# The last feed-forward with 512-column products of the hi weights, its two halves added on the way out, and its operand rows 32 and 16 bytes further apart

## The chip, the cores and the metric

One core of a Trainium2 chip runs one launch of the program. The metric is the time of that launch on the device in microseconds (us), median of several runs. The engines are named as the profile names them: PE multiplies matrices, PEld is its loading of weights, DVE and ACT work on rows of elements and read the accumulators, POOL does a little arithmetic, SP issues the transfers from memory.

## The reference

One inference step of a two-layer diffusion backbone for two groups of 128 tokens each: a context pass and a denoising step with cached keys. Both groups use the same weights, so the kernel handles them as 256 columns side by side. A layer is a mixer (latent and grouped attention in layer 0, differential attention in layer 1) and then a gated feed-forward with a width-3 convolution over positions. The change lies in the feed-forward of layer 1:

```
h = rmsnorm(x, g_norm_ffn[l]) * (1 + sc2) + sh2
u = h @ w_up                                    # 2048 -> 2 * 5632
u = up[:, :-2] * w_conv[0] + up[:, 1:-1] * w_conv[1] + up[:, 2:] * w_conv[2] + b_conv
gate, val = u[..., :D_FF], u[..., D_FF:]
x = x + gt2 * ((silu(gate) * val) @ w_down)     # 5632 -> 2048
```

All arrays are float32.

## The kernel before

**Precision by halves.** A product of float32 numbers is made of three products of a shorter kind. Every operand is split into hi (rounded, by ACT) and lo (what is left, by DVE): `split`, L247 to L249. A block of 128 by 128 weights thus exists as `wh` and `wl`, a row of activations as 256 hi columns followed by 256 lo columns. A block's share of a product is three matmuls of 256 columns (`gemm`, L356 to L381): wh with the hi columns, wh with the lo columns, wl with the hi columns, all added up in one accumulator bank `acc`. In each of them the block of weights is the stationary operand and the activations stream. Each matmul has its own weight load, so wh of a block is loaded twice.

**Rows.** The modulated activations of the feed-forward are the tile `hx`: 16 rows of 512 float32 (`operand`, L729), 2048 bytes from one row's start to the next. The gated activations are tiles `g` of 512 float32, one tile for each row.

**The feed-forward** (`ffn`, from L1501). The hidden width of 5632 is handled in two halves (NQ = 2) of 22 blocks (KQ). For each half, `up(q)` makes 44 products of 16 blocks: a gate and a value for each of 22 rows. `conv` takes a product out of its accumulator: ACT scales it and adds the bias (L1531), DVE adds the two shifted terms (L1534, L1537), both reading the accumulator. Then come silu (L1553), the product with the gate (L1554) and the split into `g`. `down(gs, q)` makes 16 products of 22 blocks, and DVE adds each into the residual `x` (`residual`, L843; the very last one in `last_residual`, L827). Four products of layer 1's first half are there before `ffn` starts (`ready`). The first products that are made inside have their first matmul widened by 32, 16, 8, 4 and 2 columns (`WIDER`).

**Weights.** SP brings 1 MB of raw weights at a time into one of three buffers; ACT rounds 8 blocks (1024 columns) into one of four `wh` buffers (L248), DVE subtracts into one of four `wl` buffers (L249). A buffer is written again when PE has used it.

**Beside it.** While the feed-forward runs, DVE also sums conditioning vectors (`feature_step`, L473): 2048 columns at a time, 0.7 of them for each product of `up`, 32 of them in this feed-forward.

**Order.** A scheduler orders the instructions of each engine when the program is built; `keep_order` pins some of them. Accumulators rotate over three banks. The order in which PE takes products is fixed once built: near the turn from `up` to `down` it interleaves products so that the last gated row is asked for late.

Of the kernel before, what the change touches and what calls it, by code (L numbers as in the profile page):

```python
# [12 lines left out]
F32R = mybir.dt.float32r  # L13
AF = mybir.ActivationFunctionType
ALU = mybir.AluOpType
# [3 lines left out]
P = 128  # L19
D = 2048  # L20
KD = D // P
T = 128
NT = 2 * T
ROW = 2 * NT
SHIFT = 320
NL = 2
# [29 lines left out]
PEW = {"heads": 1.0, "out0": 1.0, "c": 1.0}  # L56
QUIET = [4, 3, 3]
LATE = 3

EARLY = (2, 5, 8, 11, 13)  # L60
WIDER = (32, 16, 8, 4, 2)
# [33 lines left out]
def step_kernel(ctx: ExitStack, tc: tile.TileContext, A: dict):  # L95
# [45 lines left out]
    def T_(pl, shape, tag, dt=F32, bufs=None):  # L141
        kw = {} if bufs is None else {"bufs": bufs}
        return pl.tile(shape, dt, tag=tag, name=nm(tag), **kw)
# [208 lines left out]
        return [p[:, :NT] for p in ps]  # L352

    push = []

    def gemm(blocks, xh, xl, n=NT, first=0, between=None, more=None, wider=None):  # L356

# [367 lines left out]
    def home(pl, tag):  # L725

        return T_(pl, [P, (KD * 2 * UW + 127) // 128 * 128], tag, F32R)

    def operand(pl, tag):  # L729
        return home(pl, tag)[:, :KD * ROW].rearrange("p (k n) -> p k n", k=KD)  # L730

    def raw_tile(pl, tag):
        return home(pl, tag)[:, :KD * 2 * UW].rearrange("p (k n) -> p k n", k=KD)
# [1 line left out]
    def modulated(st, l, which, W, u, to, rp, tag="block"):  # L735


        ensure(l, 3 * which + 1)
        ensure(l, 3 * which)
        while later:  # L740
            later.pop(0)()
        for q in range(4):
            raw_shift(u, l, which, q)
        unit = ROWS[ada["i"]] if ada["i"] < len(ROWS) else None
        raws, got = [], {}

        def load_tile():
            raw = T_(wpool, [P, 4, 512], "araw", bufs=2)
            sp.dma_start(out=raw, in_=A["w_ada"][unit[0], unit[1], unit[2], len(raws)])
            raws.append(raw)  # L750

        def stats():
            got["r"] = stat_rstd(st, D, att_bank)

        def factor():
            got["rb"] = spread(got["r"], bank=att_bank)

        def sums(t):
            for i in range(2):
                sum_rows(t + i, raws[t + i])  # L760
            if t == 0:
                load_tile()
                load_tile()
            else:
                ada["i"] += 1
                steps.extend(ada_finish(*unit))
                steps.pop(0)()

        hooks, steps = [{6: stats, 13: factor}, {}, {}], []
        if unit:  # L770
            load_tile()
            load_tile()
            hooks[1][6] = lambda: sums(0)
            hooks[2][13] = lambda: sums(2)
        else:
            hooks.append({})
        uh, ul = (lambda k: u[:, k, :UW]), (lambda k: u[:, k, UW:])
        ps = [gemm(W.chunk(), uh, ul, UW, between=hook) for hook in hooks[:-1]]
        last = W.chunk()
        rb = got["rb"]  # L780
        rbs = T_(tmp, [P, NT], "sq", bufs=2)
        act.copy(rbs, rb)
        hx = operand(*to)
        ready = [scaled(p, rbs) for p in ps]
        for c in range(KD):
            if c % 2 == 0:
                pair = T_(rp, [P, 512], tag, bufs=3)
            row(hx, rb, l, which, c, pair[:, c % 2 * NT:(c % 2 + 1) * NT])
            if c in (5, 10):
                W.ahead(lambda i: i)  # L790
        ready.append(scaled(gemm(last, uh, ul, UW, between=hooks[-1]), rbs))
        if which == 0:
            later.extend(steps)
            steps.clear()
        return hx, ready, [(lambda: steps.pop(0)(keep_order))] if steps else []
# [704 lines left out]

    def ffn(hx, W, ready, turn, l, st):  # L1501
        xh, xl = (lambda k: hx[:, k, :NT]), (lambda k: hx[:, k, NT:2 * NT])
        wider = list(WIDER)
        long = len(ready) > 3

        def product():
            if ready:
                return ready.pop(0)
            if in_order:
                return gemm(W.chunk(), xh, xl, between=in_order.pop(0))  # L1510
            if wider:
                n = NT + wider.pop(0)
                return gemm(W.chunk(), xh, xl, more=lambda k: hx[:, k, :n])
            return gemm(W.chunk(), xh, xl)
# [3 lines left out]
        with tc.tile_pool(name=f"ffn{l}", bufs=1) as fp, banks(f"pffn{l}") as pf:  # L1518
            feat["home"], feat["pool"] = fp, pf
            feat["due"] = 0.0  # L1520
            in_order = [{}, {}] + turn + [{}]
            T_(fp, [P, SHIFT // 4], "pad")

            def conv(m):
                early = bool(ready)
                pin = keep_order if early else lambda i: i
                if len(ready) > 4 - 2 * long:
                    W.ahead(pin)
                ps = product()
                y = T_(fp, [P, NT], "cv", bufs=3)  # L1530
                pin(act.activation(y, ps, AF.Identity, scale=cw[:, 1, m:m + 1], bias=cw[:, 3, m:m + 1]))  # L1531
                y3 = y.rearrange("p (g t) -> p g t", g=2)
# [11 lines left out]
            def up(q):  # L1544
                gs = []
                for i in range(q * KQ, (q + 1) * KQ):
# [5 lines left out]
                    pump(0, rate)  # L1552
                    act.activation(gate, gate, AF.Silu)  # L1553
                    dve.tensor_tensor(out=val, in0=gate, in1=val, op=ALU.mult)  # L1554
                    g = T_(fp, [P, ROW], "g", F32R, bufs=KQ)
                    split(g[:, :NT], g[:, NT:2 * NT], val)
                    gs.append(g)
                    if i == LATE - 1:
# [3 lines left out]
            def down(gs, q):  # L1562
# [4 lines left out]
                for c in range(KD):  # L1567
                    quiet = q == NQ - 1 and c >= KD - QUIET[0]
                    fine[0] = quiet
                    if q == 0:  # L1570
                        ensure(l, 5, [c // 4])
                    ps = gemm(WD.chunk(), lambda k: gs[k][:, :NT], lambda k: gs[k][:, NT:2 * NT])
                    if l == NL - 1 and q == NQ - 1 and c == KD - 1:
                        last_residual(ps, l, 1, c, st)
                    else:
# [205 lines left out]
```

## Time and profile before

| | us |
|---|---|
| time of a launch, median of 3 runs | 2306.41 (2305.07 to 2306.84) |
| span of the profiled execution | 2305.7 |
| layer 1's feed-forward in that profile | about 1590 to 2293 |
| PE busy over the span | 2275.9 |
| DVE busy over the span | 1885.6 |
| ACT busy over the span | 1195.7 |

The span is counted from the first to the last instruction of the profiled execution; it lies 0.7 us under the median of the runs, so a difference in span can be put onto the median. A row of a profile names the source line, the engine, the operation, output<-inputs by the program's names, and shapes; "x943" is how many. Matmuls overlap, so a matmul's listed duration (276 ns) is longer than its share of the time; the share is read from the starts, or from how many begin in a stretch. A busy share of 100% for PE says that it always had a matmul under way, not that it went as fast as it can.

### The profile page before, as it was taken

Reading aid. Unit: us, or ns where it says so; the run is one execution under the profiler, and the core shown is the slowest. Engines: PE = TensorE matmul, PEld = TensorE weight load, DVE = VectorE, ACT = ScalarE, POOL = GpSimd, SP = SyncE. Lnnn points to the kernel's source line nnn. Section 1 sums busy time; section 2 is a strip of 40 time slices with the busy share of each in tenths; the row PEclk is TensorE's granted clock in tenths of the full one; section 3 lists DMA queues with packets and bytes.
Section 4 is the critical chain, followed back from the end, with each engine's and each line's share of the span. In section 5 each row is a group of like instructions: output and inputs, shape, how many; then the busy total and the mean of one; then the engine's idle time right before and its main releaser. Section 6 shows DMA issues by size and latency. Waiting matters only on the chain.

```text
span 2305.7 us, 47484 instructions
## 1 busy us (share of the span) xinstructions
PE 2275.9 (99%) x19496; PEld 2182.1 (95%) x19496; DVE 1885.6 (82%) x2973; ACT 1195.7 (52%) x1959; POOL 188.1 (8%) x238
## 2 busy tenths in 40 slices
PE   8999999999999999999999999999999999999998
PEld 6788878999999999999999999999999999999998
DVE  4667979989999999999978988898899965666654
ACT  4345555665553355555575455457555434555543
POOL 0002111300000000001130001023000000000011
PEclk9999999999999999999999999999999999999999
DMA  9987888777777777777788888776667755555553
GB/s 376 367 343 293 326 311 338 288 277 264 262 255 291 291 272 260 272 258 258 288 293 293 318 322 310 267 268 229 246 256 262 264 200 189 199 191 194 198 189 126
DMA packets 100122, 617.15 MB, mean 268 GB/s; under 512 B 10752, under 2 KB 18880, under 8 KB 33344
## 3 DMA queue, kind: packets, MB, share of 16 engines
q1 hardware_dynamic: 99904, 614.11, 72.2%
q8 instruction: 153, 2.51, 0.4%
q14 instruction: 65, 0.53, 0.1%
HBM read 609.32 MB, written 4.75 MB: 266 GB/s over the span
## 4 chain that ended last, share of the span: by engine, by line
PE 93%; DVE 3%; DMA 2%; issue 1%; POOL 1%; ACT 1%; SPq 0%; DVEq 0%; ACTq 0%; POOLq 0%
PE acc L110 86%; PE ada L110 3%; PE att L110 2%; DVE wl L249 1%; DVE hx L525 1%; DMA more<-w_ada 1%; PE att L113 1%; DMA raw<-w_out_c 0%; PE misc L110 0%; DMA araw<-w_ada 0%; DMA kvb<-w_ada 0%; POOL dev L807 0%; PE ada L113 0%; DVE rope L858 0%; ACT wh L248 0%
## 5 line engine op out<-in xcount | busy, mean ns | idle before, releaser
L110 PE MATMUL acc<-hx,wh 128*128 128x256 f32 (+1 forms) x7264 | 1255.2, 278 | 4.2 <-ACT wh L248 1.7
L248 ACT CAST wh<-raw 128x1024 fp32r<-128x1024 f32 (+1 forms) x834 | 796.6, 967 | 869.8 <-PE acc L110 736.6
L249 DVE TENSOR_TENSOR wl<-raw,wh 128x1024 fp32r<-128x1024 f32 (+1 forms) x834 | 925.4, 1126 | 246.9 <-ACT wh L248 240.2
L110 PEld LDWEIGHTS acc<-hx,wh 128*128 128x128 f32 x7264 | 1099.8, 188 | 23.2 <-ACT wh L248 8.1
L110 PE MATMUL acc<-hx,wl 128*128 128x256 f32 (+1 forms) x3632 | 1007.8, 278 | 5.3 <-DVE wl L249 5.1
L110 PEld LDWEIGHTS acc<-hx,wl 128*128 128x128 f32 x3632 | 684.5, 188 | 9.5 <-DVE wl L249 6.9
L110 PE MATMUL acc<-g,wh 128*128 128x256 f32 x2816 | 478.8, 276 | 0.0
L110 PEld LDWEIGHTS acc<-g,wh 128*128 128x128 f32 x2816 | 424.0, 188 | 0.0
L110 PE MATMUL acc<-g,wl 128*128 128x256 f32 x1408 | 388.1, 276 | 0.0
L473 DVE CUSTOM_DVE_ANT_0 junk<-araw,condb 128x2048 f32<-128x2048 f32 x128 | 294.4, 2300 | 0.0
L110 PEld LDWEIGHTS acc<-g,wl 128*128 128x128 f32 x1408 | 264.2, 188 | 0.0
L211 POOL TENSOR_TENSOR sqacc<-sqacc,sq 128x256 f32<-128x256 f32 x62 | 71.5, 1154 | 1491.1 <-ACT sq L207 1490.9
L110 PE MATMUL acc<-hxc,wh 128*128 128x256 f32 (+1 forms) x1056 | 189.3, 281 | 0.0
L110 PEld LDWEIGHTS acc<-hxc,wh 128*128 128x128 f32 x1056 | 161.9, 188 | 1.8 <-issue 1.7
L110 PE MATMUL acc<-hxc,wl 128*128 128x256 f32 (+1 forms) x528 | 146.9, 278 | 0.0
L110 PEld LDWEIGHTS acc<-hxc,wl 128*128 128x128 f32 x528 | 99.6, 189 | 0.2
L110 PE MATMUL acc<-wh,hxc 128*128 128x256 f32 (+1 forms) x512 | 95.0, 283 | 0.5 <-DVE nt L818 0.5
L1531 ACT ACTIVATE cv<-acc,convw 128x256 f32<-128x256 f32 x169 | 94.1, 557 | 0.0
L525 DVE CUSTOM_DVE_ANT_0 hx<-block,condb 128x1024 fp32r<-128x1024 f32 x65 | 79.3, 1221 | 7.3 <-DMA block<-w_ada 6.8
L1537 DVE SCALAR_TENSOR_TENSOR cv<-acc,convw,cv 128x254 f32<-128x254 f32 x169 | 81.1, 480 | 3.2
L843 DVE SCALAR_TENSOR_TENSOR x<-acc,mod,x 128x128 f32<-128x128 f32 x190 | 57.3, 344 | 31.6 <-PE acc L110 31.6
L110 PEld LDWEIGHTS acc<-wh,hxc 128*128 128x128 f32 x512 | 79.4, 188 | 3.4 <-issue 2.5
(263 smaller groups left out, 1800.4 us busy)
## 6 DMA issues: line engine op xcount, KB each, us to landing
raw<-w_up SPq DMA_DIRECT2D x176, 1024.0 KB, 4.8
araw<-w_ada SPq DMA_DIRECT2D x136, 1024.0 KB, 6.0
raw<-w_down SPq DMA_DIRECT2D x88, 1024.0 KB, 4.8
raw<-w_in_c SPq DMA_DIRECT2D x48, 1024.0 KB, 6.9
block<-w_ada SPq DMA_DIRECT2D x41, 512.0 KB, 6.8
raw<-w_in_ab SPq DMA_DIRECT2D x18, 1024.0 KB, 9.1
raw<-w_out_ab SPq DMA_DIRECT2D x16, 1024.0 KB, 7.9
raw<-w_out_c SPq DMA_DIRECT2D x16, 1024.0 KB, 7.1
```

Of the source, the lines that this page charges most:

```text
L110: return self.placed(nc.tensor.matmul(*a, **kw))
L113: return self.placed(nc.tensor.transpose(*a, **kw))
L211: eng.tensor_tensor(out=st["acc"], in0=st["acc"], in1=sq, op=ALU.add)
L248: pin(act.copy(out_hi, src))
L249: pin(dve.tensor_tensor(out=out_lo, in0=src, in1=out_hi.bitcast(F32), op=ALU.subtract))
L473: keep_order(dve.tensor_tensor_reduce(out=T_(feat["pool"], [P, D], "junk"), in1=feat["row"][:, c], in0=feat["raw"].rearrange("p g n -> p ( ...
L525: keep_order(dve.tensor_tensor_reduce(out=self.junk, in0=self.raw, in1=self.row[:, c].rearrange("p (g n) -> p g n", g=2), scale=1.0, scala ...
L843: dve.scalar_tensor_tensor(out=x[:, c, s], in0=ps[:, s], scalar=mod[:, l, 3 * which + 2, c, g:g + 1], in1=x[:, c, s], op0=ALU.mult, op1=AL ...
L1531: pin(act.activation(y, ps, AF.Identity, scale=cw[:, 1, m:m + 1], bias=cw[:, 3, m:m + 1]))
L1537: pin(dve.scalar_tensor_tensor(out=y3[:, :, :T - 1], in0=p3[:, :, 1:], scalar=cw[:, 2, m:m + 1], in1=y3[:, :, :T - 1], op0=ALU.mult, op1=A ...
```

## The change

It concerns layer 1's feed-forward alone (`wide`).

1. A new `both_gemm` takes the place of `gemm` for the 84 products of `up` that are made inside `ffn` and for the 32 products of `down`. Of each block, one matmul of 512 columns multiplies wh with the hi and the lo columns of a row, which lie next to each other, into a whole bank; one of 256 columns multiplies wl with the hi columns into the bank's first half. So the bank holds two halves that are still to be added.
2. On the way out ACT copies the second half of the bank into a tile `low`, and DVE adds the first half to it into another `low`. The convolution or the residual then reads that sum from there, not the accumulator.
3. The rows of `hx` lie 520 float32 apart (FAR = 8: 2080 bytes) in place of 512; the gated rows lie in one tile of 22 rows, 516 float32 (FARG = 4: 2064 bytes) apart, in place of 22 tiles.
4. The widened first matmuls (`WIDER`) are no longer used in this feed-forward.

```diff
+FAR = 8
+FARG = 4
...
+    def both_gemm(blocks, both, xh, between=None):
+
+
+        fixed = lambda i: keep_order(i) if between is not None else i
+        ps = T_(pacc, [P, 512], "acc")
+        last = len(blocks) - 1
+        for k, (wh, wl) in enumerate(blocks):
+            fixed(pe.matmul(ps, wh, both(k), start=(k == 0), stop=False, skip_group_check=True))
+            if between and k in between:
+                between[k]()
+            fixed(pe.matmul(ps[:, :NT], wl, xh(k), start=False, stop=(k == last), skip_group_check=True))
+        return ps
...
-    def operand(pl, tag):
-        return home(pl, tag)[:, :KD * ROW].rearrange("p (k n) -> p k n", k=KD)
+    def operand(pl, tag, far=0):
+        return home(pl, tag)[:, :KD * (ROW + far)].rearrange("p (k n) -> p k n", k=KD)
...
-        hx = operand(*to)
+        hx = operand(*to, far=FAR if (l, which) == (NL - 1, 1) else 0)
...
+        wide = l == NL - 1
...
             if in_order:
+                if wide:
+                    return both_gemm(W.chunk(), lambda k: hx[:, k, :2 * NT], xh, between=in_order.pop(0))
                 return gemm(W.chunk(), xh, xl, between=in_order.pop(0))
+            if wide:
+                return both_gemm(W.chunk(), lambda k: hx[:, k, :2 * NT], xh)
             if wider:
...
+            if wide:
+                rows = T_(fp, [P, KQ, ROW + FARG], "g", F32R)
...
+                made = wide and not ready
                 ps = product()
+                if made:
+                    low = T_(fp, [P, NT], "low", bufs=2)
+                    act.copy(low, ps[:, NT:])
+                    total = T_(fp, [P, NT], "low", bufs=2)
+                    dve.tensor_tensor(out=total, in0=ps[:, :NT], in1=low, op=ALU.add)
+                    ps = total
...
-                    g = T_(fp, [P, ROW], "g", F32R, bufs=KQ)
+                    g = rows[:, len(gs)] if wide else T_(fp, [P, ROW], "g", F32R, bufs=KQ)
...
-                    ps = gemm(WD.chunk(), lambda k: gs[k][:, :NT], lambda k: gs[k][:, NT:2 * NT])
+                    if wide:
+                        ps = both_gemm(WD.chunk(), lambda k: gs[k][:, :2 * NT], lambda k: gs[k][:, :NT])
+                        low = T_(fp, [P, NT], "low", bufs=2)
+                        act.copy(low, ps[:, NT:])
+                        total = T_(fp, [P, NT], "low", bufs=2)
+                        dve.tensor_tensor(out=total, in0=ps[:, :NT], in1=low, op=ALU.add)
+                        ps = total
+                    else:
+                        ps = gemm(WD.chunk(), lambda k: gs[k][:, :NT], lambda k: gs[k][:, NT:2 * NT])
```

What this does to the order of the built program is shown at three places. A row is one instruction or several equal ones (x2), in the order in which its engine takes them; the numbers behind names tell buffers apart, and line numbers are those of each file.

**PE, in the middle of a product of the first `up`.** Before:

```order
L110 MATMUL acc_20342<-hx_19591,wh_20334 128x256 x2
L110 MATMUL acc_20342<-hx_19591,wl_20335 128x256
L110 MATMUL acc_20342<-hx_19591,wh_20334 128x256 x2
L110 MATMUL acc_20342<-hx_19591,wl_20335 128x256
L110 MATMUL acc_20342<-hx_19591,wh_20334 128x256 x2
```

Changed:

```order
L112 MATMUL acc_20184<-hx_19591,wh_20176 128x512
L112 MATMUL acc_20184<-hx_19591,wl_20177 128x256
L112 MATMUL acc_20184<-hx_19591,wh_20176 128x512
L112 MATMUL acc_20184<-hx_19591,wl_20177 128x256
L112 MATMUL acc_20184<-hx_19591,wh_20176 128x512
```

Three matmuls of a block became two, with the same 768 columns; the order of blocks is as it was.

**DVE, in the first `up`,** where wl are the subtractions for the weights, ISA the summing of conditioning vectors (junk) and cv the convolution. Before:

```order
L249 TENSOR_TENSOR wl_20603<-raw_20600,wh_20602 128x1024
L249 TENSOR_TENSOR wl_20607<-raw_20600,wh_20606 128x1024
L1534 SCALAR_TENSOR_TENSOR cv_20526<-acc_20477,convw_14569,cv_20526 128x2x127
L249 TENSOR_TENSOR g_20464<-cv_20454,g_20464 128x256
L1537 SCALAR_TENSOR_TENSOR cv_20526<-acc_20477,convw_14569,cv_20526 128x2x127
L473 ISA junk_20530,mod_77<-araw_20458,condb_19923 128x2048
```

Changed:

```order
L1557 TENSOR_TENSOR low_20439<-acc_20404,low_20437 128x256
L251 TENSOR_TENSOR wl_20620<-raw_20617,wh_20619 128x1024
L251 TENSOR_TENSOR wl_20624<-raw_20617,wh_20623 128x1024
L1563 SCALAR_TENSOR_TENSOR cv_20441<-low_20439,convw_14569,cv_20441 128x2x127
L1566 SCALAR_TENSOR_TENSOR cv_20441<-low_20439,convw_14569,cv_20441 128x2x127
L1583 TENSOR_TENSOR cv_20441<-cv_20388,cv_20441 128x256
```

Each product has one DVE instruction more, the adding of the halves (L1557), which stands ahead of the weights' subtractions; the convolution reads its result and no longer the accumulator.

**DVE, at the end,** where x is the residual. Before:

```order
L249 TENSOR_TENSOR wl_28041<-raw_28032,wh_28040 128x512 x2
L843 SCALAR_TENSOR_TENSOR x_76<-acc_27960,mod_77,x_76 128x128 x2
L827 SCALAR_TENSOR_TENSOR x_76<-acc_28046,mod_77,x_76 128x128 x2
L219 TENSOR_SCALAR rv_28126<-misc_28120 128x1
L219 TENSOR_SCALAR rv_28126<-acc_28121 128x1
```

Changed:

```order
L251 TENSOR_TENSOR wl_26432<-raw_26423,wh_26431 128x512 x2
L1606 TENSOR_TENSOR low_26416<-acc_26369,low_26414 128x256
L858 SCALAR_TENSOR_TENSOR x_76<-low_26416,mod_77,x_76 128x128 x2
L1606 TENSOR_TENSOR low_26484<-acc_26437,low_26482 128x256
L842 SCALAR_TENSOR_TENSOR x_76<-low_26484,mod_77,x_76 128x128 x2
L221 TENSOR_SCALAR rv_26499<-misc_26493 128x1
L221 TENSOR_SCALAR rv_26499<-acc_26494 128x1
```

An adding of halves stands ahead of every residual, the last one too, behind which only the final norm comes.

## The prediction

> **What bounds the kernel now.** I read three views: the page's busy times and slices, the chain of waits over the last feed-forward, and busy time by stretches there. From the page, and then from the chain (start, length, what):
>
> ```profile
> PE 2275.9 (99%) x19496; PEld 2182.1 (95%) x19496; DVE 1885.6 (82%) x2973; ACT 1195.7 (52%) x1959; POOL 188.1 (8%) x238
> PEclk9999999999999999999999999999999999999999
> ...
> 1589.95 703.35 PE acc L110 x6196
> ```
>
> PE is the chain without a break for 703 us: no wait lies between 1590 and 2293, and the granted clock is full there. So only what a matmul takes from PE's row of them counts, and what is made late enough to break that row. The stretches of this feed-forward (PE, PEld, DVE, ACT, POOL busy, with instructions begun in them; granted clock, DMA share, GB/s):
>
> ```profile
> 1600.00:1612.00 12.00, 12.00 (x104) 12.00 (x103) 11.63 (x21) 10.43 (x17) 0.00 (x0) 1.00 0.98 352
> 1640.00:1800.00 160.00, 160.00 (x1414) 160.00 (x1413) 149.09 (x192) 85.91 (x119) 0.00 (x0) 1.00 0.73 264
> 1860.00:2160.00 300.00, 300.00 (x2650) 300.00 (x2649) 191.88 (x255) 148.39 (x192) 0.00 (x0) 1.00 0.55 194
> ```
>
> PE takes a 256-column matmul every 160/1414 = 113.2 ns (300/2650 gives the same). Between 1600 and 1612 it ran otherwise, and starts of matmuls show by how much; two timelines, of that stretch and of a usual one (start, length, engine, what):
>
> ```profile
> 1600.15 0.28 PE L110 MATMUL acc<-hx,wl 128*128 128x256 f32 x1
> ...
> 1601.21 0.28 PE L110 MATMUL acc<-hx,wl 128*128 128x256 f32 x1
> ```
> ```profile
> 1700.04 0.28 PE L110 MATMUL acc<-hx,wl 128*128 128x256 f32 x1
> ...
> 1700.72 0.28 PE L110 MATMUL acc<-hx,wl 128*128 128x256 f32 x1
> ```
>
> Three blocks lie between the first two rows, 1.06/9 = 117.8 ns for a matmul; two between the others, 0.68/6 = 113.3. Same shapes, same tiles, same clock, none waiting: 4.6 ns of the slower spacing cannot be columns. So a matmul has a part of its own, f, beside its columns. On f the change stands or falls, because the columns stay at 768 a block.
>
> **The change part by part.**
>
> *PE, three matmuls of a block made two.* There are 84 products of 16 blocks and 32 of 22: 1344 + 704 = 2048 blocks. If a 256-column matmul is f + c = 113.2, one of 512 is f + 2c = 226.4 - f, and each block gains f. No row has 512 columns of this kind. The nearest rows, again starts in timelines, are 384 columns and 258 columns:
>
> ```profile
> 219.84 0.34 PE L110 MATMUL acc<-kv_in,wl 128*128 128x384 f32 x1
> ...
> 220.36 0.34 PE L110 MATMUL acc<-kv_in,wl 128*128 128x384 f32 x1
> ```
> ```profile
> 1587.39 0.40 PE L110 MATMUL acc<-hxc,wh 128*128 128x258 f32 x2
> ...
> 1590.27 0.41 PE L110 MATMUL acc<-hxc,wh 128*128 128x258 f32 x2
> ```
>
> 384 columns cost 0.52/3 = 173.3 ns. A straight line through 256 and 384 gives 233.4 for 512, 7.0 more than two of 256: the bad end, a loss of 7.0 x 2048 = 14.3 us. 258 columns cost 2.88/24 = 120.0 (eight blocks); two columns at 113.2/256 = 0.44 account for 0.9, so at least 5.9 of the 120.0 is not columns. These two excesses, 4.6 and 5.9, are the nearest that rows come to f; the usual spacing need not be free of it either, so I take the larger, f = 5.9, and let it go up to 10 for the good end (20.5 us). With 5.9 a wide matmul takes 220.5 and a block 333.7 in place of 339.6; 2048 x 5.9 = **12.1 us gained**. The line through 384 I set aside as an end, because both lines, 256 and 384, hold an f that I don't know, and 384 may stand in its slower form as 1600 to 1612 does.
>
> The Trainium skill speaks of this in "TensorE: Matmul & The Clock Gate", section "Back-to-back issue gap": a matmul's columns at 2.4 GHz and 2.5 ns on top. As an estimate from that page 256 columns would take 109.2 and a block would gain 2.5 ns, 5.1 us in all. The trace has 113.2 at full clock, 4 more than the rule; the measurement decides, and the rule stays as the third rival's.
>
> *Rows 2080 and 2064 bytes apart.* The number of bytes read is the same. What a row's place costs, the trace shows in the 258-column products: their rows start 2064 bytes apart (516 float32), as the gated rows will, and they are the ones at 120.0. But their lo halves start 8 bytes off a multiple of 16, which no row of the change does, and 258 is no multiple of 16. I put no price on the distance in the sum and give the slow spacing to the first rival.
>
> The skill's "SBUF — State Buffer", section "SBUF: two separate sides", gives PE two reading ports, for the streamed and for the stationary operand, that do not disturb each other. [...] The trace has two spacings of one shape, 113.3 and 117.8, which it does not explain.
>
> *ACT's copy and DVE's adding.* Nearest rows (ns: least, median, most), and what DVE and ACT did from 1640 to 1800, then who waited there:
>
> ```profile
> L1141 ACT COPY proj<-acc x11: 370/373/381, 27.2 to 37.9; 128x256 f32<-128x256 f32 x11
> L1143 DVE TENSOR_TENSOR proj<-proj,acc x44: 407/420/424, 53.2 to 184.8; 128x256 f32<-128x256 f32 x44
> ```
> ```profile
> L249 DVE TENSOR_TENSOR wl<-raw,wh 128x1024 fp32r<-128x1024 f32 x59 | 70.7, 1222 | 10.4 <-ACT wh L248 10.1
> L248 ACT CAST wh<-raw 128x1024 fp32r<-128x1024 f32 x59 | 62.3, 1056 | 74.3 <-PE acc L110 62.9 <-ACT g L248 11.4
> L1537 DVE SCALAR_TENSOR_TENSOR cv<-acc,convw,cv 128x254 f32<-128x254 f32 x30 | 14.4, 479 | 0.4
> ```
>
> ACT has 74.3 of 160 us idle, so 0.37 us a product (29.5 products in the stretch, 1414/48) is covered. DVE has 10.4 + 0.4 = 10.8 us idle, 0.37 a product. Adding costs 0.42, and the product gets 16 x 5.9 ns = 0.09 shorter: DVE is short by 0.14 a product while conditioning vectors are summed, which is the whole of the first `up`, 44 products, 6 us in all. What is late next is wl, and PE behind it. What covers it is the lead: ACT waits 62.9 us for PE to free a `wh` buffer, so the four buffers are kept full. Three buffers of 8 blocks ahead are 3 x 8 x 0.34 = 8.2 us, less the cast (1.06) and the subtraction (1.22): some 5.9 us, about the shortage. Between 0 and 6 I take **1.0 us lost**. From 1860 on DVE is busy 192 of 300 us; there the adding lies in idle time. The accumulator itself is free sooner, since copy and adding read it where three instructions did; three banks of 5.3 us leave room. In DVE's and ACT's queues the weights stand behind the new pair; both wait for a product that PE has just ended, as the convolution did.
>
> *The end.* The last product is covered by nothing. In the chain:
>
> ```profile
> 2293.30 0.02 issue
> 2293.32 0.36 DVE x L827
> ```
>
> Ahead of L827 now come a copy (0.37), an adding (0.42) and two handings over (0.02 each): **0.8 us lost**. The turns from `up` to `down` lengthen by the same pair, but there PE asks for the last gated row more than a product (22 blocks, 7.3 us) after the last product of `up`.
>
> *The sum* against the profiled execution: 2305.7 - 12.1 + 1.0 + 0.8 = 2295.4. The median of the runs is 0.7 above that span: 2296.1.
>
> **Rivals.**
>
> *The slower spacing decides (slower).* PE ran 113.2 in long stretches, but 117.8 for 12 us and 120.0 where rows wander. If the new rows and the unequal matmuls keep it in the slower form throughout, f is 5.9 + 4.6 = 10.5 in it, a wide matmul takes 2 x 117.8 - 10.5 = 225.1, a block 342.9: 3.3 x 2048 = 6.8 us lost, with 1.8 for the rest **2315**. For it: the same row distance as in the 258-column rows, and no more widened first matmuls. Against: hi rows all start on multiples of 16 bytes. It loses from the point where the block's mean spacing is over 339.6.
>
> *A wide matmul costs by the line through 384 (slower).* 14.3 + 1.8 lost, **2322**. For it the one row of more than 256 columns; against it, f would be negative.
>
> *f is small (same).* If most of 113.2 is columns, f is 0 to 3: 6 us gained at the most, 1.8 given back, 2302 to 2308; with f = 2.5, **2303**. For it only that no row shows f directly. Half the blocks in the slow form ends here too: (12.1 - 6.8)/2 - 1.8 is 1 us gained.
>
> *DVE becomes the bound in the first `up`.* The whole shortage of 6 us comes through: 12.1 - 6 - 0.8, **2301**. For it DVE's 149 of 160 us; against it the lead. Still faster.
>
> That the change doesn't do what it says I give nothing: PE's order shows one matmul of 512 and one of 256 for each block.
>
> **How the numbers follow.** About 0.2%, 4.6 us, is what a measurement of this kernel can tell from no change. Forecast 0.53, DVE as the bound 0.10: faster 0.63, with some room for f near 10 inside the forecast. Small f or half the blocks: same 0.15. The slower spacing 0.17, the line 0.05: slower 0.22. Time 2296, that of the forecast; its own range is 2287 (f = 10) to 2302. The whole range goes to 2315 to take in the first rival and leaves out the line and what lies below f = 10.
>
> **What would show it.** Right: from 1640 to 1800 one wide and one narrow matmul begin in 334 ns, some 480 pairs; PE's chain stays whole; new rows of ACT near 0.37 and DVE near 0.42; about 0.8 us between the last product and L827's place. Wrong on f: pairs at 337 or more, or under 330. DVE as the bound: PE waits for wl before 1855. The slower spacing: pairs near 343 for whole products, or weight loads and matmuls whose spacing changes from row to row as in the 258-column ones.

## The result, and the profile after

The changed kernel takes **2333.78 us** (median of 4 runs, 2330.75 to 2336.07) where the kernel before takes 2306.42: ratio 1.0123, 95% interval 1.0108 to 1.0137. It is slower by 27 us; 2296 was forecast, and the time lies above the whole range. The profiled execution spans 2331.6 us, 25.9 more than that of before.

From the page of the changed kernel, busy times and granted clock; then its stretches (PE, PEld, DVE, ACT, POOL busy, with instructions; granted clock, DMA share, GB/s):

```profile
PE 2293.5 (98%) x17448; PEld 2106.9 (90%) x17448; DVE 1928.9 (83%) x3089; ACT 1230.8 (53%) x2075; POOL 190.1 (8%) x238
...
PEclk9999999999999999999999999999999999999999
```
```profile
1640.00:1800.00 160.00, 158.76 (x905) 137.79 (x904) 152.00 (x209) 89.79 (x141) 0.00 (x0) 1.00 0.70 249
1860.00:2160.00 300.00, 300.00 (x1710) 261.32 (x1710) 208.15 (x300) 156.10 (x229) 0.00 (x0) 1.00 0.56 191
```

2048 matmuls are gone, PEld has less to do, the clock is full: all as meant. But in the second stretch a pair of one wide and one narrow matmul takes 2 x 300/1710 = **350.9 ns**, where before a block of three took 3 x 300/2650 = 339.6. In the first, 453 pairs began, not the 480 that were to show the forecast right. A timeline of the changed kernel (start, length, engine, what) shows how the pair is made up:

```profile
1999.80 0.40 PE L112 MATMUL acc<-hx,wh 128*128 128x512 f32 x1
2000.03 0.28 PE L112 MATMUL acc<-hx,wl 128*128 128x256 f32 x1
2000.15 0.39 PE L112 MATMUL acc<-hx,wh 128*128 128x512 f32 x1
```

0.23 us for the wide one and 0.12 for the narrow. Over the whole feed-forward the starts give 233.0 ns (modulated rows) and 233.3 (gated rows) for 512 columns, and 117.8 and 118.5 for the 256 beside them: not 220.5 and 113.2.

From the first to the last matmul that reads `hx` or `g` the feed-forward takes 724.2 us; before it took 697.0. Of these 27.2, by the starts, some 22 are the pair (1344 x 10.3 ns over `hx`, 704 x 11.7 over `g`) and 5.2 are four stops of PE. The waits of PE in the changed kernel (what waited for what: us in total, times, longest), and then one of these stops in a timeline:

```profile
PE acc L112 <- DVE low L1606: 2.4, 1, 2.4
PE acc L112 <- DVE low L1557: 1.9, 3, 0.6
```
```profile
1693.10 2.29 DVE L488 CUSTOM_DVE_ANT_0 junk<-araw,condb 128x2048 f32<-128x2048 f32 x1
...
1694.98 0.28 PE L112 MATMUL acc<-hx,wl 128*128 128x256 f32 x1
...
1695.31 0.42 DVE L1557 TENSOR_TENSOR low<-acc,low 128x256 f32<-128x256 f32 x1
...
1695.88 0.47 PE L112 MATMUL acc<-hx,wh 128*128 128x512 f32 x1 [0.62 <-DVE low L1557]
```

The adding (L1557) stands behind 2.29 us of conditioning sums on DVE, the bank comes free late, and PE waits for the bank. The 4.3 us that these rows list count from a matmul's listed end; by the starts, counted from where the next matmul was due, the four stops are 5.2. The kernel before has no such wait in this stretch. The end, from the chain of waits of the changed kernel:

```profile
2318.59 0.38 ACT low L1604
...
2319.00 0.44 DVE low L1606
...
2319.46 0.36 DVE x L842
```

From the last matmul to the end of the span it is now 13.4 us, before 12.7.

### The profile page after: what moved, and what is told of

Its sections match the earlier page's. It is cut to its first block, busy times and chain, and to the rows that moved or that the text cites. A ratio compares the mean times of both kernels' runs of the same rounds, so it can differ in the third digit from the quotient of the medians.

```text
span 2331.6 us, 43713 instructions
## 1 busy us (share of the span) xinstructions
PE 2293.5 (98%) x17448; PEld 2106.9 (90%) x17448; DVE 1928.9 (83%) x3089; ACT 1230.8 (53%) x2075; POOL 190.1 (8%) x238
## 4 chain that ended last, share of the span: by engine, by line
PE 94%; DMA 2%; DVE 2%; ACT 1%; POOL 1%; issue 1%; SPq 0%; DVEq 0%; ACTq 0%; POOLq 0%
PE acc L112 88%; PE ada L112 3%; PE att L112 2%; DMA kvb<-w_ada 1%; DMA araw<-w_ada 1%; DMA raw<-w_in_ab 1%; DVE wl L251 1%; PE att L115 0%; DVE hx L540 0%; PE misc L112 0%; POOL dev L822 0%; PE ada L115 0%; ACT wh L250 0%; DMA block<-w_ada 0%; DVE x L1675 0%
## 5 line engine op out<-in xcount | busy, mean ns | idle before, releaser
L112 PE MATMUL acc<-hx,wh 128*128 128x256 f32 (+2 forms) x5920 | 1266.8, 305 | 6.2 <-DVE low L1557 1.9
L112 PEld LDWEIGHTS acc<-hx,wh 128*128 128x128 f32 x5920 | 945.0, 188 | 87.0 <-ACT wh L250 8.1
L112 PE MATMUL acc<-g,wh 128*128 128x256 f32 (+1 forms) x2112 | 487.0, 316 | 2.4 <-DVE low L1606 2.4
L112 PEld LDWEIGHTS acc<-g,wh 128*128 128x128 f32 x2112 | 344.0, 188 | 33.9 <-DVE low L1606 2.7
L112 PE MATMUL ada<-araw,condw 128*32 128x512 f32 (+1 forms) x608 | 76.9, 594 | 1.8 <-DMA araw<-w_ada 1.2
L112 PE MATMUL acc<-wl,hxc 128*128 128x256 f32 x256 | 71.3, 279 | 0.0
L540 DVE CUSTOM_DVE_ANT_0 hx<-more,condb 128x1024 fp32r<-128x1024 f32 x42 | 51.2, 1220 | 5.2 <-DMA more<-w_ada 4.8
```

The source lines that it names most:

```text
L112: return self.placed(nc.tensor.matmul(*a, **kw))
L540: keep_order(dve.tensor_tensor_reduce(out=self.junk, in0=self.raw, in1=self.row[:, c].rearrange("p (g n) -> p g n", g=2), scale=1.0, scala ...
```

## The experiments

The theories at the start. *Rows:* rows 2080 and 2064 bytes apart make every matmul slower. *Columns:* 512 columns are dear by themselves. *Neighbours:* ACT's and DVE's new work disturbs the reading of operands. In the course of it a fourth came up, *two forms*: a row of equal matmuls runs in a slow or a fast form, and the change has left the fast one.

**1. Prices by themselves.** Rows of matmuls alone, 96 blocks of each kind; columns, row distance, place of the weights and neighbours are varied.

```diff
+#: name; columns of a block's matmuls; elements more from row to row; neighbours busy; elements by
+#: which the weights start later; columns more in the first matmul
+T3, T2 = (256, 256, 256), (512, 256)
+STAGES = [("aa", T3, 0, 0, 0, 0), ("ab", T3, 0, 0, 0, 32), ("ac", T3, 8, 0, 0, 0), ("ad", T3, 0, 0, 16, 0),
+          ("ba", T2, 0, 0, 0, 0), ("bb", T2, 8, 0, 0, 0), ("bc", T2, 4, 0, 0, 0), ("bd", T2, 16, 0, 0, 0),
...
```

> This program leaves the whole computation out: on 17 tiles of random weights and rows it only runs rows of matmuls, 96 blocks of one pattern after the other, so that each pattern's price can be read, first with ACT and DVE idle. The changed kernel took 233 ns for a 512-column matmul and 118 for the 256-column one beside it, 351 a block, where 333.7 was forecast. Theory COLUMNS: a column of this kind costs about 0.455 ns wherever it lies, with no part for the matmul itself, so 512 columns alone and in pairs cost 226 to 234 in every pattern, rows 2048 bytes apart too, and widths from 128 to 512 lie on a line through zero. Theory ROWS: the distances of 2080 and 2064 bytes hold PE in its slower form; pairs with rows 2048 bytes apart cost about 333, those with 2080 and 2064 about 350. Theory NEIGHBOURS: ACT and DVE, reading and writing beside it, slow the stream; with both idle a pair costs 325 to 334 at all distances, with both busy 350.

Groups of instructions (line, engine, operation, tile `ps` + stage, count | busy us, mean ns):

```profile
L76 PE MATMUL psad<-x,w 128*128 128x256 f32 x288 | 34.7, 283 | 0.0
...
L76 PE MATMUL psda<-x,w 128*128 128x256 f32 x288 | 34.1, 279 | 0.0
...
L76 PE MATMUL psba<-x,w 128*128 128x512 f32 x192 | 34.1, 339 | 0.0
...
L76 PE MATMUL psbb<-x,w 128*128 128x512 f32 x192 | 33.8, 338 | 0.0
...
L76 PE MATMUL psbg<-x,w 128*128 128x512 f32 x192 | 33.4, 336 | 0.0
...
L76 PE MATMUL psca<-x,w 128*128 128x512 f32 x96 | 22.1, 391 | 0.0
...
L76 PE MATMUL pscc<-x,w 128*128 128x384 f32 x96 | 16.8, 336 | 0.0
...
L76 PE MATMUL psce<-x,w 128*128 128x256 f32 x96 | 11.5, 279 | 0.0
...
L76 PE MATMUL pscf<-x,w 128*128 128x192 f32 x96 | 10.9, 274 | 0.0
...
L76 PE MATMUL pscg<-x,w 128*128 128x128 f32 x96 | 10.9, 275 | 0.0
```

A stage's busy time holds its matmuls' spacings and one listed length; (34.1 - 0.28)/287 = 117.8 ns. So three matmuls of 256 take 117.8 each, 353.4 a block, with busy neighbours (da) and without (the starts in stage aa from its ninth block on; the first ones, right at the program's start, are slower). The pair is the same to 0.1 ns with them busy (db, dc) as idle (ba, bb): *neighbours* falls. All 96 x 3 matmuls of stage da are in what was the odd, slower spacing of the kernel before; its 113.3 does not occur in this run at all. The pair takes 353 with rows 2048 apart (ba), 351 with 2080 (bb), and 347 at best (bg, weights 32 bytes later). Alone, 512 columns take 228.5 ns, 384 columns 173.3, 256 columns 118, and 192 and 128 columns about 111 both. The starts give 146.7, 173.3 and 200.0 for 320, 384 and 448: 0.417 ns a column and 13.3 beside them. What lies beside the columns is not the same at every width: 11.1 for 256 columns, 13.3 for 320 to 448, 15 for 512 alone and, by the starts, 20 for 512 beside a matmul of 256 (ba; 15 in bg).

**2. Rows 2048 bytes apart.** The change with both distances taken back.

```diff
-FAR = 8
-FARG = 4
+FAR = 0
+FARG = 0
```

> The changed kernel with its rows at the old distance, 2048 bytes for both tiles; the 512-column matmuls and the adding of halves stay. ROWS: the pair falls from 351 to about 334 ns, the time from 2334 to about 2298. COLUMNS and NEIGHBOURS: the pair stays at 347 to 355 and the time within 10 us of 2334.

**2340.0 us**, ratio 1.0145 (1.0128 to 1.0162). A stretch:

```profile
1860.00:2160.00 300.00, 300.00 (x1701) 260.60 (x1700) 206.01 (x296) 153.82 (x225) 0.00 (x0) 1.00 0.56 187
```

2 x 300/1701 = 352.7 a pair, as stage ba has it. For the pair the distances are a gain of 2 ns; *rows* does not explain why it is dear.

**3. The distances alone.** The kernel before, three matmuls and widened first ones, with rows 2080 and 2064 apart.

```diff
-        wide = l == NL - 1
+        wide = False
...
-                    g = rows[:, len(gs)] if wide else T_(fp, [P, ROW], "g", F32R, bufs=KQ)
+                    g = rows[:, len(gs)] if l == NL - 1 else T_(fp, [P, ROW], "g", F32R, bufs=KQ)
```

> The kernel before, with three 256-column matmuls a block and nothing to add, but with rows 2080 and 2064 bytes apart as in the change. ROWS: matmuls go from 113.2 to about 118 ns, the block from 340 to 353, and the time to about 2333, nearly all of the loss. COLUMNS: if the slower form has nothing to do with rows, the block stays at 340 and the time at 2306, within 5 us.

**2334.23 us**, ratio 1.0118 (1.0103 to 1.0133): the whole loss, without a wide matmul.

```profile
1860.00:2160.00 300.00, 300.00 (x2539) 300.00 (x2538) 182.05 (x240) 139.23 (x180) 0.00 (x0) 1.00 0.53 186
```

3 x 300/2539 = 354.5 a block. PE never stops. The distances take the fast spacing away from three matmuls, though the pair is none the worse for them.

**4. The change with two halves of 256.** Only the width is taken back: wh with the hi and wh with the lo columns as two matmuls into the bank's halves, distances and adding kept.

```diff
-            fixed(pe.matmul(ps, wh, both(k), start=(k == 0), stop=False, skip_group_check=True))
+            fixed(pe.matmul(ps[:, :NT], wh, both(k)[:, :NT], start=(k == 0), stop=False, skip_group_check=True))
+            fixed(pe.matmul(ps[:, NT:], wh, both(k)[:, NT:], start=False, stop=False, skip_group_check=True))
```

> The changed kernel with each 512-column matmul made as two of 256 columns into the two halves of the bank; distances of rows and the adding of halves stay. ROWS: three matmuls at about 118, block 353, time 2334 to 2340. COLUMNS: the block goes to 340 to 346, since only width set the price, time 2312 to 2325; what then remains over 2306 is the adding of halves, its wait in PE (5 us in the changed kernel's profile) and the end (0.7 us).

**2337.32 us**, ratio 1.0131 (1.0115 to 1.0146); blocks at 354.5 again:

```profile
1860.00:2160.00 300.00, 300.00 (x2539) 300.00 (x2539) 207.05 (x299) 154.21 (x228) 0.00 (x0) 1.00 0.53 189
```

Against the change, the width is worth 3.5 us: 3.6 ns a block, 7 us, less some 3 us by which PE stops longer in the change. Against experiment 3, adding and halves cost 3.1 us (the widened matmuls are gone here too; in experiment 3 they bring no fast form). So *columns* falls as the cause of the loss: a wide matmul is cheaper than two narrow ones of the same form, though by 3.6 ns and not by the 11 that a narrow one has beside its columns. What the kernel before has is another form.

**5. What brings the fast form.** Rows of matmuls again; in each of six runs of 16 blocks one matmul is wider, by 32, 16, 8, 4, 2 and 0 columns (`push`), in some stages by the same number each time.

```diff
+            if push and k == 0 and j == (1 if two else 0):
+                c += push[b // 16]
```

> Nothing of the reference is computed: rows of matmuls only, 96 blocks of each kind, on a quiet chip, rows 2048 bytes apart unless said. In each run of 16 blocks one matmul is 32, 16, 8, 4, 2 or 0 columns wider than the others. Two theories. TWO FORMS: three 256-column matmuls have a slow form (117.8 ns each) and a fast one (113.3), and a wider matmul can turn the one into the other, as the kernel before has it at 1613 and 1624 us. Then some stretch of a stage with three matmuls goes on at 113.3 after its wider matmul, and not at rows 2064 or 2080 apart. PLACE: the 113 ns of the kernel before come from something else of it (its addresses, its weight buffers), and every stage with three matmuls stays at 117.8 but for the wider matmul itself. For the pair of 512 and 256: if it has a fast form too, a stretch after a wider matmul is at 220 and 113, together 333 (what the prediction took); if it has none, all stages stay between 346 and 354. Pairs whose second matmul is always 264, 272 or 288 columns wide cost 3.3, 6.7 or 13.3 ns more in the pair if nothing else changes, 354 to 364; under 345 if they sit in a fast form.

Three stretches of stage aa in timelines, after the matmuls that are wider by 8, by 4 and by 2 columns (start, length from the first start to the last end, and count):

```profile
24.29 5.22 PE L80 MATMUL psaa<-x,w 128*128 128x256 f32 x43
```
```profile
29.82 5.15 PE L80 MATMUL psaa<-x,w 128*128 128x256 f32 x44
```
```profile
35.28 5.34 PE L80 MATMUL psaa<-x,w 128*128 128x256 f32 x44
```

With the listed length of 0.28 taken off: 4.94/42 = 117.6, 4.87/43 = **113.3**, 5.06/43 = 117.7. One row, one shape, one set of addresses, full clock, nothing else on the chip's engines: the matmul of 260 columns turned it into the fast form, and the one of 258 out of it again. That is the two forms. No other stage with three matmuls got there: not with 32, 16, 8, 4 or 2 columns more each time, not with rows 2064 or 2080 apart. Of the twelve stages in which the pair's narrow matmul was widened in this way none was under 346 ns; always 264, 272 or 288 columns made a pair of 353 to 365. One stage with the pair in another order, 512, 256, 256, 512, had 345.

**6. No widening.** The kernel before without its five widened matmuls in the last feed-forward.

```diff
-        wider = list(WIDER)
+        wider = list(WIDER) if l < NL - 1 else []
```

> The kernel before, without the five widened matmuls at the start of the last feed-forward; nothing else. TWO FORMS, got into by the widened matmuls: that feed-forward stays at 117.8 ns a matmul, 353.4 a block, and the time is 2306 + 2044 x 13.6 ns = about 2334, as long as the kernel with the distances alone. FORM OF THE PLACE: the fast form comes from rows 2048 bytes apart and would come by itself at the first tile's end; then the time stays at 2304 to 2309.

**2331.22 us**, ratio 1.0110 (1.0095 to 1.0126).

```profile
1860.00:2160.00 300.00, 300.00 (x2549) 300.00 (x2548) 182.42 (x241) 140.34 (x181) 0.00 (x0) 1.00 0.53 186
```

3 x 300/2549 = 353.1 a block, and the starts give the same from beginning to end. Five matmuls, 62 columns too wide together, are worth 25 us.

**7. The adding alone.** The kernel before with the copy (scaled by zero, so that sums stay) and the adding.

```diff
+                    act.activation(low, ps, AF.Identity, scale=0.0)
+                    dve.tensor_tensor(out=total, in0=ps, in1=low, op=ALU.add)
```

> The kernel before with its three matmuls, widened first ones and rows 2048 bytes apart, and with the change's two added operations for each of the same products: a ScalarE copy of 256 columns out of the bank (scaled by zero, so that the sum stays what it was) and a VectorE addition. ADDING IS CHEAP: the spacing stays at 113.3 ns, and the time rises by the end's 0.7 us and the 0 to 5 us of TensorE's idle time, 2307 to 2312. ADDING COSTS THE FORM: later evictions make TensorE stop, and a stop throws it out of the fast form; then blocks are at 353 and the time is 2325 to 2340.

The five runs fall in two groups: 2313.24 and 2314.34, and 2328.63 to 2330.79 (median 2328.63, ratio 1.0085, 1.0055 to 1.0115). The profile is of the 2314.34. Its stretches and, in a timeline, two of its stops:

```profile
1660.00:1690.00 30.00, 30.00 (x257) 30.00 (x256) 28.90 (x41) 16.97 (x26) 0.00 (x0) 1.00 0.67 239
...
1860.00:2160.00 300.00, 300.00 (x2649) 300.00 (x2648) 215.52 (x312) 161.94 (x240) 0.00 (x0) 1.00 0.56 197
```
```profile
1656.58 0.28 PE L110 MATMUL acc<-hx,wl 128*128 128x256 f32 x1
...
1656.92 0.28 PE L110 MATMUL acc<-hx,wl 128*128 128x256 f32 x1
1657.03 0.45 PE L110 MATMUL acc<-hx,wh 128*128 128x256 f32 x2
1657.32 0.28 PE L110 MATMUL acc<-hx,wl 128*128 128x256 f32 x1
...
1657.67 0.28 PE L110 MATMUL acc<-hx,wl 128*128 128x256 f32 x1
```
```profile
1696.54 0.28 PE L110 MATMUL acc<-hx,wl 128*128 128x256 f32 x1
1697.25 0.50 PE L110 MATMUL acc<-hx,wh 128*128 128x256 f32 x2 [0.43 <-DVE low L1535]
```

Blocks of 0.34 us up to 1656.92, one of 0.40, then blocks of 0.35: a stop of some 0.06 us turned the row into the slow form, and it stayed there until a stop of about 0.6 at 1696.54 turned it back. At 1769.2, after a delay of 0.015 us, and at 1808.7, after another stop of 0.6, the same happened again. But not every stop does it: after delays of 0.017 us at 1713.7 and 0.019 at 1746.5 the row was back in the fast form within three blocks, and after a stop of 0.8 at 1751.9 within two. From 1860 to 2160 the row is fast throughout (3 x 300/2649 = 339.8 a block). (The widened first matmul had brought the fast form as before.) Both expectations hold in part: the adding costs the fast form, but in this run not for good. The slow group lies where a row that is mostly in the slow form would be; those runs have no profile here, so that is inferred.

**8. A better pair?** Other orders of a block's matmuls, other distances and places, on rows of matmuls.

```diff
+TURN3, TURN2 = O3 + ((1, 2), (1, 1), (1, 0)), O2 + ((1, 1), (1, 0))
...
+WIDE2, WIDE4 = ((0, 0), (1, 0), (0, 1), (1, 1)), tuple((b, j) for j in (0, 1) for b in range(4))
+WIDE16 = tuple((b, j) for j in (0, 1) for b in range(16))
```

> Nothing of the reference is computed: rows of matmuls only, 96 blocks of each kind, on a quiet chip, in other orders of a block's matmuls (every second block backwards, two wide ones before two narrow ones, and so on), with other row distances and other places of the weights. For the pair of 512 and 256, which so far had 345 to 354 ns in 30 kinds of stage: NO FAST PAIR: none comes under 343 ns. THE ORDER DECIDES: some order or place gives 333 to 340, and the change could then be made as fast as the kernel before or faster. For three of 256: if the fast form is one of two ways in which the same row can run, three matmuls with two blocks widened by 16 and 8 columns, or three by 32, 16 and 8, stay at 113.3 ns to the end of their stage; an order or place in which every matmul takes 113.3 without any widening would make the widening needless.

```profile
L92 PE MATMUL psab<-x,w 128*128 128x256 f32 (+1 forms) x288 | 34.1, 279 | 0.0
...
L92 PE MATMUL psca<-x,w 128*128 128x512 f32 x192 | 33.3, 335 | 0.0
L92 PE MATMUL psda<-x,w 128*128 128x512 f32 x192 | 33.3, 335 | 0.0
```

The quickest pairs have rows 2048 apart and the orders 512, 256, 256, 512 (ca), 512, 512, 256, 256 (da), or sixteen wide ones and then sixteen narrow (de): at 2 x (33.3 - 0.28)/191 = 345.8 (345.0 to 345.8 by the starts): *no fast pair*. For three matmuls the expectation was put wrongly: 32, 16 and 8 columns stay slow here as they did in experiment 5, where the fast form came only with the fourth widening, the one by 4 that is left out here; 16 and 8 (stage ab) and other orders stay slow too. And 4 columns alone did nothing in experiment 5. So it isn't one widening as such that does it; what it meets in the row must count too, and no run shows what. Nor is the slow spacing one number: with the weights 16 bytes later (af) three matmuls run at 116.7 ns each, with 8 or 24 bytes (ae, ag) at 120.0. No stage came to 113.3 by itself.

A limit of *no fast pair*: rows of matmuls alone do not show what 32 columns do in the kernel (experiment 11), and no run has the change with a widened matmul. What can be said is that no kind of pair that ran came below about 345 ns.

**9. The best pair in the kernel.** The change with rows 2048 apart and every second block's two matmuls in the other order.

```diff
+            if k % 2:
+                two.reverse()
```

> The change with rows 2048 bytes apart, and with every second block's two matmuls in the other order (512, 256, 256, 512), the pair that the rows of matmuls had quickest: 345.0 ns. Theory TWO FORMS, with no fast one for the pair: 345 ns in the kernel too, 8.3 ns under the 353.3 of the change with rows 2048 bytes apart, 2048 x 8.3 = 17 us less than its 2340, so 2321 to 2325: the best that the wide matmul has, and still slower than the kernel before by 15 to 19. Rival, the pair in the kernel does not follow the rows of matmuls: 350 or more, 2332 to 2341. Rival, a pair that comes into a fast form in the kernel: 333 to 340, 2298 to 2312.

**2325.44 us**, ratio 1.0092 (1.0075 to 1.0109).

```profile
1860.00:2160.00 300.00, 300.00 (x1733) 263.25 (x1732) 213.82 (x307) 160.42 (x234) 0.00 (x0) 1.00 0.57 191
```

2 x 300/1733 = 346.2 a pair; the launch is 8 us quicker than the change and 20 slower than before: for the pair the rows of matmuls tell the kernel's spacing, and their quickest pair does not reach 339.6.

**10. Only the gated rows further apart** (2064 bytes), everything else as before.

```diff
-FAR = 8
+FAR = 0
```

> The kernel before with its three matmuls and widened first ones; only the gated rows 2064 bytes apart, the modulated rows 2048 as before. If the distance of the rows that are being read decides at each moment, the 1344 blocks over modulated rows stay at 340 ns and the 704 over gated rows go to 355: 704 x 15 = 10.6 us, 2316 to 2318. If the fast form, once lost, does not come back without a widened matmul, the first up part (about 660 blocks) stays fast and all that follows the first down part is slow, 353 to 355 over some 1400 blocks: 2325 to 2328. If the distance does nothing by itself: 2304 to 2309.

**2324.98 us**, ratio 1.0089 (1.0074 to 1.0104). First `up`, first `down`, second `up`, last `down`:

```profile
1640.00:1800.00 160.00, 160.00 (x1415) 160.00 (x1413) 149.10 (x195) 85.36 (x119) 0.00 (x0) 1.00 0.71 260
1830.00:1900.00 70.00, 70.00 (x595) 70.00 (x594) 46.92 (x57) 26.10 (x25) 0.00 (x0) 1.00 0.59 211
1920.00:2120.00 200.00, 200.00 (x1701) 200.00 (x1700) 126.44 (x169) 99.01 (x134) 0.00 (x0) 1.00 0.53 187
2180.00:2290.00 110.00, 110.00 (x934) 110.00 (x934) 58.10 (x79) 49.50 (x66) 14.20 (x12) 1.00 0.53 188
```

339.2, 352.9, 352.7 and 353.3 ns a block (each count holds two or three matmuls that began ahead of the stretch, so the starts give up to 2 ns more in the short ones). The second `up` reads the same rows with the same shapes as the first, and is slow: here the fast form, once lost, does not come back by itself. (The gated rows also lie in one tile in place of 22, as in the change; no run takes that apart from the distance.)

**11. One widened matmul** (288 columns) in place of five.

```diff
-        wider = list(WIDER)
+        wider = list(WIDER)[:1 if l == NL - 1 else None]
```

> The kernel before with only the first of the five widened matmuls of the last feed-forward (288 columns); the other four have 256. ONE STEP: that matmul alone turns the row of matmuls into the fast form, and nothing turns it back: 113.3 ns from 1613 us on, 2304 to 2309. CHANCE: the later four are needed to hold it, or the form depends on the moment at which the row starts: 117.8 ns from somewhere on, up to the 2331 of the kernel without any widening; runs of one kernel may then differ by up to 25 us.

**2304.94 us** (10 runs, 2302.38 to 2306.91), ratio 0.9996 (0.9987 to 1.0006): the kernel before. Its timeline around that matmul:

```profile
1607.07 0.28 PE L110 MATMUL acc<-hx,wl 128*128 128x256 f32 x1
...
1608.13 0.28 PE L110 MATMUL acc<-hx,wl 128*128 128x256 f32 x1
1608.25 0.41 PE L110 MATMUL acc<-hx,wh 128*128 128x288 f32 x2
...
1608.85 0.28 PE L110 MATMUL acc<-hx,wl 128*128 128x256 f32 x1
...
1609.53 0.28 PE L110 MATMUL acc<-hx,wl 128*128 128x256 f32 x1
```

Blocks of 1.06/3 = 0.353 us before it, of 0.68/2 = 0.34 behind it, and so to the end, as a late stretch shows (3 x 300/2650 = 339.6):

```profile
1860.00:2160.00 300.00, 300.00 (x2650) 300.00 (x2649) 192.18 (x253) 148.87 (x193) 0.00 (x0) 1.00 0.55 194
```

**12. Gated rows 2176 bytes apart**, so that each row starts at the same place within 128 bytes.

```diff
-FARG = 4
+FARG = 32
```

> The kernel before with its three matmuls and widened first ones and the modulated rows 2048 bytes apart; the gated rows 2176 bytes apart (32 float32 more), where 2064 bytes gave 2325. BYTES WITHIN 128: what throws the row out of the fast form is that a row starts elsewhere within 128 bytes; at 2176 each starts at the same place, so the blocks over gated rows stay at 340 ns: 2304 to 2309. ANY DISTANCE BUT 2048: the blocks from the first down part on are at 353 to 355, 2323 to 2327.

**2313.00 us**, ratio 1.0033 (1.0020 to 1.0045): between the two expectations.

```profile
1830.00:1900.00 70.00, 70.00 (x601) 70.00 (x601) 46.75 (x57) 26.17 (x26) 0.00 (x0) 1.00 0.59 211
1920.00:2120.00 200.00, 200.00 (x1763) 200.00 (x1762) 133.01 (x178) 103.10 (x140) 0.00 (x0) 1.00 0.54 192
```

Over gated rows 349.4 ns a block (350.1 by the starts); over the modulated rows that follow 340.3, the fast form again. Neither theory as put holds: at 2176 the block is slow while such rows are read, but the fast form is there again behind them, which at 2064 it was not. Why, no run here shows.

## Why the prediction was wrong

**The step that failed is the first term, "PE, three matmuls of a block made two", -12.1 us, through what it was worked out from.** The forecast saw both spacings, 117.8 and 113.3, and that 4.6 ns of the difference cannot be columns. It then took 113.2 as what a matmul of this kernel costs, and 5.9 ns of it as what a matmul is rid of when two become one. Two things in this failed.

First, the form. That f was near for the fast form (with 0.417 ns a column, 113.3 holds 6.6 beside its 256 columns) is luck: 5.9 is what a slower row had on top of 113.2, not a part of it. And the fast form belongs to a row of three equal matmuls, 2048 bytes from row to row, that a widened matmul has brought into it (experiments 3, 6, 10, 11). Without these the fixed part is about 11 ns for 256 columns. The pair was costed by the form that the change itself abolishes.

Second, f was taken to be the same whatever the width. It is 15 ns for 512 columns alone and 20 in the change's pair. Of the 17 ns that a pair missed its price by, 4.6 are the narrow matmul's slow form (117.8), about 4 the wide one's price with the slow form's f of 11.1 (213.3 + 11.1 = 224.4 in place of 220.5), and the other half, 8.6, is the wide matmul's larger part of its own (233.0). Measured: 351 ns in place of 333.7, a loss of 22 us in place of a gain of 12.1.

**"Rows 2080 and 2064 bytes apart: no price"** failed too. Alone they cost 27.8 us (experiment 3), all of it by the loss of the fast form. For the wide pair by itself they are a gain of 2 ns a block. The prediction gave the risk to its first rival and held against it that all hi rows start on multiples of 16 bytes; experiment 12 shows that even rows a multiple of 128 bytes apart are slower at another distance than 2048. The Trainium skill, "SBUF — State Buffer", section "SBUF: two separate sides", has the streamed and the stationary operand read through ports that are independent of each other. That says nothing of where rows lie. The rows of this case have one shape at 113.3 and 117.8, and 120.0 where only the weights lie 64 bytes further on (experiment 1, stage ad), so the operands' places do matter.

**That `WIDER` falls away was not costed at all.** It stood in the list of the change and, as half a sentence, in the first rival. Experiment 6 puts it at 25 us, experiment 11 at one matmul. Either of the two edits, distances or no widening, is enough for the whole loss; they don't add up.

**The rivals.** The line through 384 columns had the wide matmul right (233.4, measured 233.0), and kept 113.2 for the narrow one. That it was right is in part luck, since it joins a 256 of the fast form to a 384 with no such form on record; from 117.8 the same line gives 228.8, which is 512 columns alone (228.5), not in the pair. The slower spacing had the narrow one right (117.8), and with f = 10.5 made the wide one 225.1. What came is both at once, 350.8, which stood in no case. The note that 384 columns may stand in the slower form fits experiment 1, where 384 take the same 173.3 in a run without any 113.3; a quicker 384 was not seen, so it isn't shown. Of the rule in the Trainium skill, "TensorE: Matmul & The Clock Gate", section "Back-to-back issue gap", the columns at 2.4 GHz (0.417 ns) agree with experiment 1; its 2.5 ns on top, which the page gives for a matmul by itself, does not hold in these rows, with 6.6 to 20 measured here.

**ACT's copy and DVE's adding: the shortage was right, its path was not.** 1.0 us was taken, 0 to 6 allowed; PE's stops are 5.2. The lead in weights held: PE waited for no `wl` buffer. It waited for the accumulator instead, which the text had as "free sooner": 1.9 us idle where the adding stood behind conditioning sums and 2.4 in the first `down`, behind two subtractions. Experiment 7 shows what such a stop can cost a row of three matmuls besides: its form. **The end** was right, 0.8 predicted and 0.7 measured.

The sum by what was measured, from the first to the last matmul of the feed-forward: 697.0 before; 726.4 with the distances (the form lost); 728.5 with adding and halves; 724.2 with the width, the change.

## What to carry to other kernels

A spacing that a tuned kernel shows is a property of its whole row of matmuls, not of one; before costing an edit by it, look for the same shape at another spacing in the same trace, and find what divides the two, because the edit may abolish just that. An odd line, such as a few matmuls that are made wider for no product, should be costed by taking it out alone before anything is built beside it. And fewer instructions for the same columns pay only as far as they stay in the same form: here two narrow matmuls, made one, gained 4 ns in the slow form while the fast form was worth 13.

## What the runs showed of the hardware

- One row of 256-column float32 matmuls, each with its own weights, at full clock, can last in two forms, 117.8 and 113.3 ns. A matmul 32 columns wider (1608.25 in experiment 11) or a stop of 0.06 us (1657.03 in experiment 7) turned one into the other; a stop of 0.8 us (1751.9 there) did not. But 32 columns, which did it in the kernel, did not in rows of matmuls alone (experiment 5), where 4 columns behind 32, 16 and 8 did. What in the chip the two are, and which moment leads to which, stays open. With the weights at other places the same row ran at 116.7 or 120.0 (experiment 8).
- Below 256 columns hardly anything is gained: 192 and 128 columns take some 111 ns alone, 256 in the fast form 113.3.
- Operands' places move a pair of 512 and 256 between 346.7 and 353.4 ns with nothing else running; turning every second block's order is worth 8 ns at rows 2048 bytes apart (353 to 345).
